# A hybrid attention block on Trainium2: x loaded with features first, the first norm's factor applied to the products

## The chip, the cores and the metric

The kernel runs on one core of one Trainium2 chip. The metric is the device time of one execution in microseconds (us). Of the kernel before, three runs were timed: median 1287.97 us, from 1284.92 to 1291.63. One more execution was taken with the profiler; its own time was 1289.89 us.

## The reference

x has 1024 tokens of 1024 features. What is computed, cut to what matters here:

```
h    = x * rsqrt(mean(x*x, features) + eps) * norm_mix        # first RMSNorm
proj = h @ w_in                                               # 1024 x 3384
qa, ka, va, qi, ki, wi, qb, kb, vb, gdown, ogate = split(proj)
score = sum_h relu(qi_h . ki) * wi_h ; keep the 256 best keys of each query (block causal)
o_a  = softmax(qa . ka + bias, over the kept keys) @ va       # 8 heads of 64
o_b  = gated linear attention of qb, kb, vb with gates from gdown; RMSNorm; * silu(ogate)
x    = x + concat(o_a, o_b) @ w_out
x    = x + (silu(n(x) @ w_gate) * (n(x) @ w_up)) @ w_down     # n: second RMSNorm
out  = RMSNorm(x) * norm_final
```

The factor rsqrt(...) is one number per token and `norm_mix` is one number per feature, so the product of a token's row with `w_in` can be scaled by the token's factor before or after the matmul.

## The kernel before

Every product that must be exact in fp32 is made of three matmuls of a fast fp32 form: an operand is split into a high part (ScalarE, a rounding copy) and a low part (the difference, VectorE or GpSimd), and `mm3` (lines 371 to 374) issues high x high, high x low, low x high. SBUF is handed out in 41 pages of 4 KB per partition, PSUM in four banks (`ps`) and two double banks (`pl`); further small buffers are `hp` and `kb`.

The order of the work is written by a planner, `Flow` (lines 139 to 228), that runs while the program is built. Each piece of work is a thread (a generator) with a rank. It yields what it waits for (an event, a slot, a planned time `At(t)`) or an engine with a cost in ns. The planner always takes the request that can start earliest on its engine; among those within 20 ns it takes the thread of lowest rank. It then lets that thread emit its instruction. The planned times are used for this order alone: on the chip each engine runs its instructions in the order in which they were emitted, each waiting for its real operands. DMAs are all issued by SyncE (SP), in their emitted order too.

The start (lines 405 to 429) issues x in eight tiles of 128 tokens (512 KB each), an identity matrix, the first norm's weight, and the columns of `w_in` for ki, wi and gdown, gathered into one page `wms` by three strided DMAs. Then:

- `first_norm` (482): sum of squares of a token tile (ScalarE or VectorE), the factor (GpSimd), and x scaled in place (VectorE, line 489).
- `hidden` (505): TensorE transposes each 128x128 block of scaled x (line 522). `split_hidden` (492) turns each 128 features x 512 tokens into a page `hT` with high and low part (lines 496 and 498), times `norm_mix`.
- `small_weights` (531) splits `wms` into `wm`.
- `main` (2271) orders TensorE: `misc(0)`, `index_queries(0)`, `misc(1)`, `index_queries(1)`, and then the projections `proj_t` and `proj_f`: vb, og, qkb, qa, va, qa, ka. The number in brackets is the half of the tokens. Results leave PSUM through the functions `evac_...`.
- Beside the projections run `scores` and `choose` (the index scores and a bit by bit search for the 256th score, on VectorE and ScalarE), `bias`, `decays` and `gla`; after ka the softmaxes, the output projection, the FFN.

Weights come through the class `Weights` (lines 231 to 322): three staging buffers `st` (256 KB each), a DMA into a free one, the high part by ScalarE (line 257) into a page, the low part by GpSimd (line 262), which frees the buffer. `Weights.load()` fetches into the staging buffers at once, outside the planner; nothing calls it in the kernel before. `Weights.flow` hands what is staged to the planner's threads, without a planned landing time; a fetch made inside the planner gets one:

```python
for st in self.staged:                            # line 284, when the planner's clock is 0
    staged.put(st)
...
staged.put(self.fetch(), 3200)                    # line 295, in loads()
...
st = yield staged                                 # lines 299 to 302, in highs(), rank 5
yield self
yield ACT, act(HB) + 42
split.put((st, self.high(st)))
```

Of the kernel before, what the change touches and what calls it, by code (L numbers as in the profile page):

```python
# [58 lines left out]
def dve(n):  # L59
    return n / 0.96 + 68  # L60
# [265 lines left out]
def block_kernel(ctx: ExitStack, tc: tile.TileContext, a: dict, out: bass.AP, dbg=None):  # L326
# [78 lines left out]
    xs = {}  # L405

    def load_x(i):
        xs[i] = page([P, D], F32, "x")
        nc.sync.dma_start(xs[i], x[i * P:(i + 1) * P, :])

    load_x(0)
    mats = cst.tile([P, 6, P], F32, name="mats")
    nc.sync.dma_start(mats[:, 0:1, :], a["c_mats"][:, 0:1, :])
    ident, tri, flip, cmask = (mats[:, i, :] for i in range(4))
    cmi = mats[:, 4:6, :].rearrange("p a n -> p (a n)").bitcast(I32)
    load_x(1)
    nrm = cst.tile([P, 2, KT], F32, name="nrm")
    wms = page([P, KT, P], F32, "wms")
    nc.gpsimd.memset(wms, 0.0)
    wv = w_in.rearrange("(k p) n -> p k n", p=P)  # L420
    with nc.allow_non_contiguous_dma("small"):
        nc.sync.dma_start(nrm[:, 0, :], a["norm_mix"].rearrange("l (k p) -> p (l k)", p=P))
        load_x(2)
        load_x(3)
        nc.sync.dma_start(wms[:, :, 32:72], wv[:, :, C_KI:C_KI + 40])
        nc.sync.dma_start(wms[:, :, 0:32], wv[:, :, C_KI:C_KI + 32])
        nc.sync.dma_start(wms[:, :, 96:112], wv[:, :, C_GD:C_GD + 16])
    for i in range(4, 8):
        load_x(i)

    def more_loads():

        todo = [(mats[:, 1:, :], a["c_mats"][:, 1:, :]), (wgu[96:112, :], w_gu),
                   (bgt, row_bc(a["b_gate"], 256)), (gnb, row_bc(a["gla_norm"], 512)), (tab, a["rel_bias"]),
                   (nrm[:, 1, :], a["norm_ffn"].rearrange("l (k p) -> p (l k)", p=P))]
# [13 lines left out]
    junk_v = cst.tile([P, S], BF16, name="junk_v")  # L449

# [18 lines left out]
    pg = Slots(fl, NPG - NT - 1)  # L469
    hp, kb, ps, pl = (Slots(fl, n) for n in (NHP, NKB, 4, 2))  # L470
    fl.free[DMA] = 16500.0
# [5 lines left out]
    hT = {}  # L477

# [3 lines left out]
    def first_norm(i):  # L482
        yield At((4500.0, 6050.0, 8650.0, 10000.0, 14000.0, 15250.0, 16700.0, 18200.0)[i])
        yield (ACT, act(S) + 140) if i % 2 == 0 else (DVE, dve(S))
        ss = sumsq(xs[i], i % 2 == 0)
        yield POOL, 730
        r = rstd_of(ss, 1, D)
        yield DVE, 660
        nc.vector.tensor_scalar(xs[i], xs[i], r, None, op0=ALU.mult)
        ev("xn", i).set()  # L490

    def split_hidden(hf, d, b, give):
# [3 lines left out]
        nc.scalar.activation(t[:, 0, :], b, AF.Copy, scale=nrm[:, 0, d:d + 1])  # L496
        yield DVE, dve(HB) + 60
        nc.vector.scalar_tensor_tensor(t[:, 1, :], b, nrm[:, 0, d:d + 1], f32(t[:, 0, :]),
                                       op0=ALU.mult, op1=ALU.subtract)
        if give is not None:  # L500
            give.give()
        hT[d, hf] = t
        ev("hT", d, hf).set()

    def hidden(hf):

        step = KT if hf == 0 else 2
        for d0 in range(0, KT, step):
            bs = []
            if hf == 0:  # L510
                for _ in range(4):
                    yield ps
                    bs.append((bank("tp"), ps))
            while len(bs) < step:
                yield pl
                w = wide("tp")
                bs += [(w[:, :HB], None), (w[:, HB:], pl)]
            for j in range(4):
                yield ev("xn", hf * 4 + j)
                for d in range(d0, d0 + step):  # L520
                    yield PE, pe(P, 2)
                    nc.tensor.transpose(bs[d - d0][0][:, j * P:(j + 1) * P], xs[hf * 4 + j][:, d * P:(d + 1) * P],
                                        ident)
            for d in range(d0, d0 + step):
                fl.spawn(split_hidden(hf, d, *bs[d - d0]), 0.01 * d)
        pg.give(n=4)
# [4 lines left out]
    def small_weights():  # L531
        yield At(11200.0)
        for _ in range(2):
            yield pg
        yield ACT, act(S)
        wm.extend(page([P, KT, P], F32R, "wm") for _ in range(2))
        nc.scalar.activation(wm[0], wms, AF.Copy)
        yield DVE, dve(S)
        nc.vector.tensor_tensor(wm[1], wms, f32(wm[0]), op=ALU.subtract)
        pg.give()  # L540
        ev("wm").set()

    def evac_misc(hf, b):
        o = slice(hf * HB, (hf + 1) * HB)
        if hf == 0:
            for _ in range(2):
                yield pg
            kw.extend((page([P, S], F32R, "K4"), page([P, S], F32, "wg")))
        K4, wg = kw
        yield ACT, act(HB)  # L550
        nc.scalar.activation(K4[0:64, o], b[0:64, :], AF.Copy)
        yield DVE, dve(HB)
        nc.vector.scalar_tensor_tensor(K4[64:128, o], b[0:64, :], 1.0, f32(K4[0:64, o]),
                                       op0=ALU.mult, op1=ALU.subtract)
        yield ACT, act(HB)
        nc.scalar.activation(wg[64:128, o], b[64:128, :], AF.Copy)
        ps.give()
# [4 lines left out]
    def misc(hf):  # L562
        yield ps
        yield ev("wm")
        b = bank("misc")
        for k in range(KT):
            yield ev("hT", k, hf)
# [55 lines left out]
    def index_queries(hf):  # L623
# [3 lines left out]
        for _ in range(2):  # L627
# [1729 lines left out]
```

## Time and profile before

| what | value |
|---|---|
| median of three runs | 1287.97 us (1284.92 to 1291.63) |
| profiled execution | 1289.89 us, span 1288.1 us |
| TensorE (PE) busy | 1243.2 us, 97% of the span |
| VectorE (DVE), ScalarE (ACT), GpSimd (POOL) busy | 933.7, 600.6, 394.5 us |
| TensorE's mean granted clock | 0.985 |
| DMA | 232 MB, 180 GB/s over the span |

The span runs from the first to the last instruction; the execution's own time is 1.8 us more. TensorE has a granted clock of 1.00 or 0.50 (2.4 or 1.2 GHz); a window's number is the mean. An idle gap is shown in square brackets with the instruction that ended it.

### The profile page before, as it was taken

To read this page: it belongs to the slowest core of one execution; us is meant where nothing else is said; L and a number is where in the kernel's file an instruction comes from. 1 tells how busy PE (TensorE), PEld (TensorE's weight loads), DVE (VectorE), ACT (ScalarE), POOL (GpSimd) and SP (SyncE) were. 2 spreads that over 40 slices of the span, in tenths; PEclk is the share of its full clock that TensorE was granted. 3 is DMA by queue.
4 is the path that set the end of the run, shared out by engine and by line. 5 is a ranking of instruction groups with operands and counts; after the bars stand their busy time and mean duration, and the time that the engine had idled before them with its cause. 6 is when DMAs were issued, how large, how long until landed. Compare 5 with 4: busy or idle time off the path is not lost. (4 is left out here: it accounts for less than half of the span.)

```text
span 1288.1 us, 17923 instructions
## 1 busy us (share of the span) xinstructions
PE 1243.2 (97%) x6074; PEld 1022.6 (79%) x6074; DVE 933.7 (72%) x1739; ACT 600.6 (47%) x1113; POOL 394.5 (31%) x375
## 2 busy tenths in 40 slices
PE   6999999999999999899989999999999999999997
PEld 5878878767787998778868787878888888888885
DVE  6389988979964998843688887768778653335875
ACT  4467777634524787621344444444444332222333
POOL 5324335523401544310103334334333120000340
PEclk8999999979999999999989999999999999999999
DMA  6653221334563437683015777767665479555664
GB/s 212 191 150 123 74 74 42 131 138 152 178 221 100 114 85 201 190 270 129 34 61 184 273 245 258 254 246 261 229 219 205 133 258 379 180 196 190 225 238 164
DMA packets 124909, 232.06 MB, mean 180 GB/s; under 512 B 14297, under 2 KB 72465, under 8 KB 124817
## 3 DMA queue, kind: packets, MB, share of 16 engines
q1 hardware_dynamic: 124816, 230.91, 54.4%
q8 instruction: 48, 0.79, 0.3%
q14 instruction: 45, 0.36, 0.1%
HBM read 148.02 MB, written 82.85 MB: 179 GB/s over the span
## 5 line engine op out<-in xcount | busy, mean ns | idle before, releaser
L1626 POOL TENSOR_TENSOR w<-raw,w 128x512 fp32r<-128x512 f32 x60 | 85.3, 1424 | 214.2 <-ACT w L1766 182.3
L1766 ACT ACTIVATE w<-raw 128x512 fp32r<-128x512 f32 x132 | 81.4, 626 | 54.3 <-DMA d_wd<-wd 15.0
L760 DVE TENSOR_SCALAR_CACHE_REDUCE junk_v<-acc,thr 128x768 bf16<-128x768 f32 (+3 forms) x128 | 103.7, 810 | 2.0
L262 POOL TENSOR_TENSOR w<-st,w 128x512 fp32r<-128x512 f32 x52 | 73.4, 1422 | 75.5 <-ACT w L257 73.3
L767 ACT ACTIVATE junk_a<-acc,thr 128x1024 bf16<-128x1024 f32 x64 | 73.4, 1146 | 46.2 <-DVE thr L784 37.5
L2102 DVE TENSOR_TENSOR da<-U,da 128x512 fp32r<-128x512 f32 x54 | 43.1, 799 | 53.7 <-ACT da L2100 53.5
L2100 ACT ACTIVATE da<-U 128x512 fp32r<-128x512 f32 x54 | 33.7, 630 | 98.8 <-PE da L2156 33.2
L372 PE MATMUL pj<-w,hT 128*128 128x512 f32 x192 | 79.2, 412 | 0.0
L2031 ACT ACTIVATE wd<-wd 128x512 fp32r<-128x512 f32 x77 | 48.3, 629 | 62.1 <-DMA d_wd<-wd 28.1
L373 PE MATMUL pj<-w,hT 128*128 128x512 f32 x192 | 75.9, 395 | 0.0
L374 PE MATMUL pj<-w,hT 128*128 128x512 f32 x192 | 75.8, 395 | 0.0
L372 PE MATMUL pf<-hT,w 128*128 128x512 f32 x192 | 75.8, 395 | 0.0
L1347 POOL TENSOR_SCALAR pb<-pb,sume 128x384 f32<-128x384 f32 (+3 forms) x64 | 47.7, 751 | 89.9 <-DVE sume L1345 74.1
L374 PE MATMUL pf<-hT,w 128*128 128x512 f32 x192 | 74.8, 389 | 0.0
L373 PE MATMUL pf<-hT,w 128*128 128x512 f32 x192 | 74.8, 389 | 0.0
L1807 PE MATMUL fb<-hc,w 128*128 128x512 f32 x176 | 69.5, 395 | 3.9 <-DVE gt L1842 2.5
L1808 PE MATMUL fb<-hc,w 128*128 128x512 f32 x176 | 69.2, 393 | 3.8 <-DVE hc L1629 3.8
L1808 PE MATMUL fc<-hc,w 128*128 128x512 f32 x176 | 69.5, 395 | 2.4 <-DVE hc L1629 2.4
L1807 PE MATMUL fc<-hc,w 128*128 128x512 f32 x176 | 69.1, 392 | 0.4 <-DVE gt L1861 0.4
L2156 PE MATMUL da<-db,da 128*128 128x512 f32 x176 | 68.7, 390 | 0.7 <-DVE da L2102 0.7
L1626 POOL TENSOR_TENSOR wd<-wd 128x512 fp32r<-128x512 f32 x33 | 49.8, 1511 | 63.7 <-ACT wd L2031 55.9
L2154 PE MATMUL da<-db,da 128*128 128x512 f32 x176 | 68.6, 390 | 0.6 <-ACT da L2100 0.6
(315 smaller groups left out, 3643.7 us busy)
## 6 DMA issues: line engine op xcount, KB each, us to landing
d_wd<-wd SPq DMA_DIRECT2D x77, 512.0 KB, 3.5
db<-d_wd SPq DMA_DIRECT2D x77, 512.0 KB, 4.3
st<-w_in SPq DMA_DIRECT2D x52, 256.0 KB, 2.8
raw<-w_ffn_gate SPq DMA_DIRECT2D x22, 512.0 KB, 5.2
raw<-w_ffn_up SPq DMA_DIRECT2D x22, 512.0 KB, 4.5
wd<-w_ffn_down SPq DMA_DIRECT2D x44, 256.0 KB, 4.8
d_ux<-gt SPq DMA_DIRECT2D x9, 512.0 KB, 2.6
d_uy<-gt SPq DMA_DIRECT2D x9, 512.0 KB, 3.5
```

What stands on the lines that cost most here:

```text
L262: (eng or self.nc.gpsimd).tensor_tensor(w[:, 1, :], st, f32(w[:, 0, :]), op=ALU.subtract)
L372: mm(ps, lh, rh, start=first, stop=False)
L373: mm(ps, lh, rl, start=False, stop=False)
L374: mm(ps, ll, rh, start=False, stop=last)
L760: v.tensor_scalar(junk_v[:, :w], acc[ts[i]], col, float(S - TOPK), op0=ALU.is_ge, op1=ALU.subtract, accum_out=cnt[:, i:i + 1])
L767: nc.scalar.activation(junk_a[:, :NA[t]], acc[t], AF.Sign, bias=thf[:, nv:], scale=-1.0, accum_out=cnt[:, nv:])
L1626: nc.gpsimd.tensor_tensor(dst, src, high, op=ALU.subtract)
L1766: nc.scalar.activation(w4[:, 0], src, AF.Copy)
L1807: mm(b, w[:, 0, kk], h[:, 0, :], start=first, stop=False, skip_group_check=True)
L1808: mm(b, w[:, 0, kk], h[:, 1, :], start=False, stop=False, skip_group_check=True)
L2154: mm(bs[t], l[:, 0, tt], r[:, 0, :], start=first, stop=False, skip_group_check=True)
L2156: mm(bs[t], l[:, 1, tt], r[:, 0, :], start=False, stop=last, skip_group_check=True)
```

## The change

x is given to the kernel a second time, transposed (`c_xt`, features first), the small weights are given already gathered (`c_wm`), and both norm weights as rows (`c_norms`). The pages `xT` are split straight into `hT`, times `norm_mix`; there are no transposes and no scaling of x before the products. The tokens' factors are made later, from x in its old layout, which is still loaded. They are applied where results leave PSUM: as a per-partition scale where tokens are rows (`evac_t`, `evac_va`), and by a multiplication with `R` where tokens are columns. `R` holds the factors of all tokens along the free axis, the same in every partition; `rows` makes it with eight plain fp32 matmuls of a diagonal and the identity. Three weight tiles are fetched by `W.load()` at the start.

```diff
+    def load_xt(k, hf):
+        if k % 2 == 0:
+            t = page([P, 2, HB], F32, "xT")
+            xT[k, hf], xT[k + 1, hf] = t[:, 0, :], t[:, 1, :]
+        nc.sync.dma_start(xT[k, hf], a["c_xt"][k * P:(k + 1) * P, hf * HB:(hf + 1) * HB])
...
+    load_xt(0, 0)
+    nc.sync.dma_start(nrm, a["c_norms"])
+    load_wm(0)
+    for k in range(1, 4):
+        load_xt(k, 0)
+    load_wm(1)
+    for k in range(4, KT):
+        load_xt(k, 0)
+    nc.sync.dma_start(mats[:, 0:1, :], a["c_mats"][:, 0:1, :])
+    W.load()
...
-        yield At(26000.0)
+        yield ev("x", NT - 1)
...
-    fl.free[DMA] = 16500.0
+    fl.free[DMA] = 12000.0
     W.flow(fl, pg, R_W)
...
+    def split_hidden(k, hf):
+        if hf == 0:
+            yield At(4500.0 + 650.0 * (k + (k > 3)))
+        else:
+            yield ev("xt", k)
         yield pg
         yield ACT, act(HB) + 42
         t = page([P, 2, HB], F32R, "hT")
-        nc.scalar.activation(t[:, 0, :], b, AF.Copy, scale=nrm[:, 0, d:d + 1])
+        nc.scalar.activation(t[:, 0, :], xT[k, hf], AF.Copy, scale=nrm[:, 0, k:k + 1])
...
+    def load_tokens():
+        W.limit = 4
+        for k in range(KT):
+            if k % 2 == 0:
+                yield pg
+            yield DMA, 650
+            load_xt(k, 1)
+            ev("xt", k).set(2500)
+        for i in range(NT):
+            yield pg
+            yield DMA, 1300
+            xs[i] = page([P, D], F32, "x")
+            nc.sync.dma_start(xs[i], x[i * P:(i + 1) * P, :])
+            ev("x", i).set(2500)
+        W.limit = 8
...
+    def rows():
+        yield pl
+        w = wide("rows")
+        for hf in range(2):
+            yield hp
+            m = half([P, 4, P], F32, "rcol")
             for j in range(4):
+                i = 4 * hf + j
+                yield ev("rs", i)
+                yield DVE, 250
+                nc.vector.tensor_scalar(m[:, j, :], ident, 0.0, rs[:, i:i + 1], op0=ALU.mult, op1=ALU.add)
+                yield PE, 350
+                mm(w[:, i * P:(i + 1) * P], m[:, j, :], ident, start=True, stop=True)
+            hp.give()
+            yield ACT, act(HB)
+            o = slice(hf * HB, (hf + 1) * HB)
+            nc.scalar.activation(R[:, o], w[:, o], AF.Copy)
+            ev("R", hf).set()
+        pl.give()
...
+    def small_weights(i):
+        yield At((5150.0, 7750.0)[i])
...
     def evac_misc(hf, b):
+        yield ev("R", hf)
+        yield DVE, dve(HB)
+        nc.vector.tensor_tensor(wg[:, o], b, R[:, o], op=ALU.mult)
+        ps.give()
         yield ACT, act(HB)
-        nc.scalar.activation(K4[0:64, o], b[0:64, :], AF.Copy)
+        nc.scalar.activation(K4[0:64, o], wg[0:64, o], AF.Copy)
...
     def index_queries(hf):          # half 1 now takes a double bank (pl), not two of ps
     def evac_qi(hf, c, b):          # multiplies by R first, then splits the SBUF copy
...
     def evac_qa(hf, c, b):
-        nc.scalar.activation(t[:, 0, :], b, AF.Copy, scale=-0.125)
-        yield DVE, dve(HB)
-        nc.vector.scalar_tensor_tensor(t[:, 1, :], b, -0.125, f32(t[:, 0, :]), op0=ALU.mult, op1=ALU.subtract)
-        ps.give()
+        nc.vector.scalar_tensor_tensor(q, b, -0.125, R[:, hf * HB:(hf + 1) * HB], op0=ALU.mult, op1=ALU.mult)
+        ps.give()
+        yield ACT, act(HB)
+        nc.scalar.activation(t[:, 0, :], q, AF.Copy)
+        yield POOL, pool2(HB)
+        nc.gpsimd.tensor_tensor(t[:, 1, :], q, f32(t[:, 0, :]), op=ALU.subtract)
...
     def evac_qkb(hf, c, b):
-        nc.scalar.activation(dst[i][:, o], b, AF.Copy, scale=0.125 if c < 2 else 1.0)
+        nc.vector.scalar_tensor_tensor(dst[i][:, o], b, 0.125 if c < 2 else 1.0, R[:, o], op0=ALU.mult, op1=ALU.mult)
...
     def evac_ka(hf, c, b):
+        nc.vector.tensor_tensor(kf, b, R[:, o], op=ALU.mult)
+        ps.give()
         yield ACT, 2 * act(HB)             # two high parts, now from kf in SBUF
...
+            nc.vector.tensor_tensor(k[q, o], kf[r, :], f32(k[r, o]), op=ALU.subtract)
...
+    for i in range(2):
+        fl.spawn(small_weights(i), -1.5)
+    for hf in range(2):
+        for k in range(KT):
+            fl.spawn(split_hidden(k, hf), -1 + hf + 0.01 * k)
+    fl.spawn(load_tokens(), 6)
     for i in range(NT):
+        fl.spawn(first_norm(i), 0.2 + 0.01 * i)
+    fl.spawn(rows(), 0.4)
+    fl.spawn(free_rows(), 1)
```

`first_norm` now waits for `ev("x", i)` and ends with the factor in `rs`; `free_rows` gives R's page back after the last evacuation that reads it.

## Rows read from the trace of the kernel before

**Rows 1.** Section 1 of the page: busy us, share of span, instructions.

```profile
PE 1243.2 (97%) x6074; PEld 1022.6 (79%) x6074; DVE 933.7 (72%) x1739; ACT 600.6 (47%) x1113; POOL 394.5 (31%) x375
```

**Rows 2.** Waits of TensorE: waiter <- releaser: us in total, times, longest.

```profile
PE misc L372 <- DVE hT L498: 2.5, 1, 2.5
...
PE lg L1324 <- DVE mn L1337: 3.1, 2, 2.9
...
PE pk L1102 <- DVE att L1121: 2.9, 1, 2.9
```

**Rows 3.** Windows: busy us of each engine, granted clock, DMA share, GB/s.

```profile
core 0: us, PE busy (x) PEld busy (x) DVE busy (x) ACT busy (x) POOL busy (x), PEclk, DMA share, GB/s
...
0.00:8.54 8.54, 0.00 (x1) 0.01 (x1) 2.08 (x4) 2.43 (x3) 3.98 (x10) 1.00 0.70 230
...
13.00:18.00 5.00, 2.45 (x16) 2.10 (x16) 4.23 (x6) 3.75 (x8) 2.21 (x5) 0.90 1.01 402
...
17.61:23.75 6.14, 6.14 (x15) 4.79 (x16) 6.14 (x9) 5.18 (x10) 3.09 (x5) 0.50 0.32 105
...
250.00:260.00 10.00, 5.91 (x34) 3.89 (x33) 9.89 (x24) 5.71 (x12) 3.97 (x4) 1.00 0.34 117
...
260.00:280.00 20.00, 20.00 (x99) 13.49 (x100) 12.43 (x36) 5.79 (x10) 3.20 (x4) 0.66 0.21 75
```

**Rows 4.** Timeline of TensorE: start us, us, engine, line, operation, count.

```profile
17.61 0.79 PE L372 MATMUL misc<-hT,wm 128*128 128x512 f32 x1 [2.55 <-DVE hT L498]
...
31.63 1.31 PE L522 MATMUL tp<-mats,x 128*128 128x128 f32 x10 [0.43 <-DVE x L489]
...
34.97 1.06 PE L522 MATMUL tp<-mats,x 128*128 128x128 f32 x8
...
35.79 0.48 PE L372 MATMUL misc<-hT,wm 128*128 128x512 f32 x1
...
52.42 0.39 PE L372 MATMUL pj<-w,hT 128*128 128x512 f32 x1
...
227.24 1.05 PE L1028 MATMUL bc<-mats,la 128*128 128x128 f32 x8
...
228.05 0.48 PE L372 MATMUL pf<-hT,w 128*128 128x512 f32 x1
```

**Rows 5.** Timeline of SyncE's DMA issues, start of the program.

```profile
0.72 0.40 SPq L409 DMA_DIRECT2D x<-x  x1
1.18 0.42 SPq L413 DMA_DIRECT2D mats<-c_mats  x1
...
12.06 15.66 SPq L247 DMA_DIRECT2D st<-w_in  x6
```

**Rows 6.** Timeline of ScalarE: its first wait for x.

```profile
4.52 1.06 ACT L460 ACTIVATE junk_a<-x 128x1024 bf16<-128x1024 f32 x1 [2.52 <-DMA x<-x]
```

**Rows 7.** Groups of instructions by line: count, busy us, mean ns, idle before.

```profile
L257 ACT ACTIVATE w<-st 128x512 fp32r<-128x512 f32 x68 | 41.6, 629 | 9.9 <-DMA st<-w_in 5.3 <-DMA st<-w_out 4.3
...
L262 POOL TENSOR_TENSOR w<-st,w 128x512 fp32r<-128x512 f32 x52 | 73.4, 1422 | 75.5 <-ACT w L257 73.3 <-PE pj L374 1.7 <-PE pf L374 0.2
...
L867 DVE SCALAR_TENSOR_TENSOR spillq<-pf,spillq 128x512 fp32r<-128x512 f32 x8 | 5.2, 684 | 0.3 <-ACT spillq L865 0.2
```

**Rows 8.** Timeline of VectorE and GpSimd: L784 alone, then beside GpSimd.

```profile
250.01 0.15 DVE L784 SCALAR_TENSOR_TENSOR thr<-bit,thr 128x3 int32<-128x3 int32 x1
...
256.08 1.47 POOL L888 TENSOR_TENSOR spillv<-spill,spillv 128x512 fp32r<-128x512 f32 x1
...
256.32 1.24 DVE L784 SCALAR_TENSOR_TENSOR thr<-bit,thr 128x3 int32<-128x3 int32 x1
```

**Rows 9.** Line 829, the finished masks: duration ns, first and last start.

```profile
L829 DVE TENSOR_SCALAR acc<-sign x6: 347/588/1664, 257.5 to 368.8; 128x1024 f32<-128x1024 bf16 x2, 128x384 f32<-128x384 bf16 x1, 128x768 f32<-128x768 bf16 x1, 128x512 f32<-128x512 bf16 x1
```

**Rows 10.** Timeline of VectorE where the softmaxes begin.

```profile
402.60 0.56 DVE L1337 CUSTOM_DVE_ANT_0 pb<-lg,acc 128x384 f32<-128x384 f32 x1 [7.42 <-PE lg L1331]
...
405.17 2.79 DVE L1257 SCALAR_TENSOR_TENSOR K<-pf,K 64x512 fp32r<-64x512 f32 x4
```

More of the change, by code (lines that the diff above doesn't have):

```diff
@@ L449, in block_kernel @@
     junk_v = cst.tile([P, S], BF16, name="junk_v")
+    rs = cst.tile([P, NT], F32, name="rs")
     def rstd_of(ss, n, width):
@@ L502, in split_hidden @@
[L502 to L517, printed above, removed]
-            for j in range(4):
[L519 to L526, printed above, removed]
@@ L529, in block_kernel @@
-    wm, kw = [], []
[L531 to L541, printed above, removed]
+        hT[k, hf] = t
+        if k % 2:
+            pg.give()
+        ev("hT", k, hf).set()
@@ new lines, in load_tokens, with first_norm @@
+    def load_tokens():
[13 more added lines that the diff above has]
+        W.limit = 8
+    def first_norm(i):
+        yield ev("x", i)
+        yield (ACT, act(S) + 140) if i % 2 == 0 else (DVE, dve(S))
+        ss = sumsq(xs[i], i % 2 == 0)
+        pg.give()
+        yield POOL, 730
+        r = small([P, 1], F32, "rstd", 4)
+        nc.gpsimd.tensor_scalar(r, ss, 1.0 / D, EPS, op0=ALU.mult, op1=ALU.add)
+        nc.gpsimd.tensor_tensor(rs[:, i:i + 1], r, mhalf[:, 0:1], op=ALU.pow)
+        ev("rs", i).set()
@@ new lines, in block_kernel @@
+    R = page([P, S], F32, "rows")
+    def rows():
[4 more added lines that the diff above has]
+            m = half([P, 4, P], F32, "rcol")
+            for j in range(4):
+                i = 4 * hf + j
[10 more added lines that the diff above has]
+        pl.give()
@@ new lines, in free_rows @@
+    def free_rows():
+        for hf in range(2):
+            for c in range(4):
+                yield ev("ka", hf, c)
+                yield ev("qa", hf, c)
+                yield ev("qk", hf, c)
+        pg.give()
+    wm, kw = [], []
+    def small_weights(i):
+        yield At((5150.0, 7750.0)[i])
+        if i == 0:
+            for _ in range(2):
+                yield pg
+            wm.extend(page([P, KT, P], F32R, "wm") for _ in range(2))
+        o = slice(4 * i, 4 * i + 4)
+        yield ACT, act(HB)
+        nc.scalar.activation(wm[0][:, o, :], wms[:, o, :], AF.Copy)
+        yield DVE, dve(HB)
+        nc.vector.tensor_tensor(wm[1][:, o, :], wms[:, o, :], f32(wm[0][:, o, :]), op=ALU.subtract)
+        if i:
+            pg.give()
+        ev("wm", i).set()
@@ L626, in index_queries @@
         bs = []
-        for _ in range(2):
-            yield ps
-            bs.append(bank("qi"))
+        if hf == 0:
+            for _ in range(2):
+                yield ps
+                bs.append(bank("qi"))
+        else:
+            yield pl
+            w = wide("qi")
+            bs = [w[:, :HB], w[:, HB:]]
         for k in range(KT):
@@ L1247, in evac_ka @@
         yield ev("ka page", c)
+        yield hp
+        yield DVE, dve(HB)
+        kf = half([P, HB], F32, "kf")
+        nc.vector.tensor_tensor(kf, b, R[:, o], op=ALU.mult)
+        ps.give()
         yield ACT, 2 * act(HB)
@@ L2307, in main @@
         yield from down()
+    for i in range(2):
+        fl.spawn(small_weights(i), -1.5)
+    for hf in range(2):
+        for k in range(KT):
+            fl.spawn(split_hidden(k, hf), -1 + hf + 0.01 * k)
+    fl.spawn(load_tokens(), 6)
     for i in range(NT):
[L2310 to L2313 removed]
+        fl.spawn(first_norm(i), 0.2 + 0.01 * i)
+    fl.spawn(rows(), 0.4)
+    fl.spawn(free_rows(), 1)
     fl.spawn(more_loads(), 2)
@@ L2340, in _constants, with _layouts @@
     }
+def _layouts(inputs):
+    w = np.asarray(inputs["w_in"])[0].reshape(KT, P, -1).transpose(1, 0, 2)
+    wm = np.zeros((P, KT, P), np.float32)
+    wm[:, :, 0:32] = w[:, :, C_KI:C_KI + 32]
+    wm[:, :, 32:72] = w[:, :, C_KI:C_KI + 40]
+    wm[:, :, 96:112] = w[:, :, C_GD:C_GD + 16]
+    gains = [np.asarray(inputs[n])[0].reshape(KT, P).T for n in ("norm_mix", "norm_ffn")]
+    return {
+        "c_xt": np.ascontiguousarray(np.asarray(inputs["x"])[0].T),
+        "c_wm": wm,
+        "c_norms": np.ascontiguousarray(np.stack(gains, axis=1)),
+    }
 def kernel(**inputs):
@@ L2349 @@
     arrays.update(_constants())
+    arrays.update(_layouts(inputs))
     aps = {n: nc.dram_tensor(n, v.shape, mybir.dt.from_np(v.dtype), kind="ExternalInput").ap()
```

95 lines of the change are left out of this document (36 added, 59 removed).

## The prediction

> **What bounds the kernel now.** I read the page's busy shares first: TensorE is busy for 1243.2 of 1288.1 us [rows 1], so all other engines only matter where they make it wait or slow. Next the waits of TensorE and the windows: some 45 us of idle time, in few places, and each longer gap is followed by a stretch at half clock. The head is the largest: the first projection matmul starts at 17.61 us, after a last wait of 2.55 us for `hT` [rows 4], and the next 6.14 us run at a granted clock of 0.50 [rows 3]. From there to the first matmul of vb (`pj`, 52.42 us) TensorE is full but for 0.43 us before a batch of transposes [rows 4]. Behind that the notable gaps are 2.9 us at `pk` for `att` in the stretch 250 to 260 us, and 2.9 us at `lg` where the softmaxes begin [rows 2]. So I count on TensorE's timeline: when does the first matmul start, what lies between it and `pj`, and which later gaps change.
>
> **The first matmul.** Before, its chain is x, sum of squares, factor, scaling, transposes, split. Now it is transposed x, `norm_mix` and half the small weights, then one split each. The data would allow an early start: x's first tile of 0.524 MB is read at 4.52 us [rows 6], a tile now is half that, and small weights and `norm_mix` come right behind; split and first matmul would follow at about 6 us.
>
> I don't expect that, because of the order on ScalarE. `W.load()` puts three tiles into staging before the planner starts. `flow` hands them over with no landing time, so for the planner they are there at 0. The first three high parts (L257) therefore can start at 0, 0.58 and 1.16 us of planned time; the first `split_hidden` is held until 4.5 and `small_weights` until 5.15. The planner takes the earliest, so these three stand first in ScalarE's order. On the chip they wait for the weights, which are the last of the first 15 DMAs, and all splits stand behind them.
>
> When does the third land? Ahead of it and with it: 8 tiles of x and 3 of weights of 0.262 MB, 2 parts of small weights of 0.262 MB, identity and norms 0.07 MB: 3.48 MB. Issuing is no limit: 15 issues at 0.46 us (0.72 to 1.18) [rows 5] end at 7.6 us. With 0.524 MB at 4.5 us and then the rate of large rows, 402 GB/s in the stretch 13 to 18 us [rows 3]: 4.5 + 2.96/0.402 = 11.9 us. Then on ScalarE the third high part, the first split and half of the small weights, 0.63 us each (L257) [rows 7]: 13.8, with hops 14.0 us. VectorE's low parts (0.68 us) [rows 7] are ready for the second and third matmul. So the first matmul moves from 17.61 to 14.0: **-3.6 us**. Bounds: 402 is the fastest stretch here; at the 230 GB/s of the first 8.54 us [rows 3], which hold the start and strided loads, the start would be at 4.5 + 12.9 + 2.1 = 19.5, +1.9. I take the fast end, since the transfers are now of its kind (long rows, none strided).
>
> The Trainium skill ("DMA: Bandwidth & Descriptors", section Where 436 GB/s comes from) says that HBM gives a core about 358 GB/s, and that this binds for HBM to SBUF. By that, as an estimate, the third tile lands at 12.8 and the gain is 2.7; the row shows 402 for such loads, and the row decides.
>
> From the first matmul on: per 128 features ScalarE needs 0.63 us, TensorE at half clock three matmuls, and before it ran 15 in 6.14 us [rows 3], 1.23 us for three. So it isn't starved, and it warms up in the same time: no change.
>
> **From the first matmul to `pj`.** Before: 52.42 - 17.61 = 34.8 us. Out go the 32 transposes of the second half, four times eight at 35.79 - 34.97 = 0.82: 3.3 us, and the wait of 0.43 [rows 4]. In come the 8 fp32 products of `rows`: four such take 228.05 - 227.24 = 0.81, so 1.6 us [rows 4]. About as many breaks in the stream as before, 6 against 8; 0.2. Sum **-1.9 us**; bounds -3.7 (products free in a gap) and 0 (each costs twice). `pj` then starts at 46.9.
>
> **What could be late there.** SP's order is x half 0, three weight tiles, then three more weight tiles (planned at 12.0 us, rank 5 before rank 6), x half 1, the token tiles. The three wait for a free buffer, hence for GpSimd's low parts: 11.2 + 3 x 1.42 [rows 7] = 15.5 us, and everything behind waits with them, as the six fetches of L247 held SP for 15.66 us before [rows 5]. Half 1 (2.1 MB) is there by 23 us, needed from 28 (14.0 + the old 8.5 of `misc(0)` and 5.7). A seventh fetch holds the last of half 1 and the token tiles until GpSimd's fourth low part, about 21; the token tiles (4.2 MB) then land by 35, the last factor follows at 37, and the product of its tile stands at some 88% of `index_queries(1)`, near 44: 7 us of cover. R's first half is made near 39, and the first two banks for `pj`, held until the multiplication with R, come free by 42. If this cover went, TensorE would wait at `rows` or at `pj`; that is a rival. The evacuations that wait for R hold up VectorE's and ScalarE's order behind them (scores, weights of vb), which need the products of `index_queries(1)` anyhow.
>
> **Behind `pj`.** The multiplications with R add on VectorE 2 (misc), 4 (qi), 8 (qkb) and 8 (ka) of about 0.68 us [rows 7], 15 us, and 8 diagonals, below 2; the 8 scalings of x are gone. qa keeps its number on VectorE and adds 8 subtractions of 1.42 on GpSimd. ScalarE loses as many copies as qkb and misc drop. PSUM banks are held shorter (one operation, not two). VectorE's long work beside the projections is the search; its last mask starts at 368.8 [rows 9] and the first softmax needs one at 402.60 [rows 10]: 33 us of cover for 15, so nothing, and the full 15 if the cover were gone. One place isn't covered: at 405.17 four low parts of ka take 2.79 us while TensorE waits for a softmax's bank [rows 2, 10]. Two multiplications more in that burst: **+1.4 us**; bounds 0 (they fall into the idle time before) and 2.9 (the gap doubles). Moving qa's low part to GpSimd has a price: L784 takes 0.15 us alone and 1.24 beside a GpSimd subtraction [rows 8]. Eight of them delay VectorE by 0 to 9 us, under the same cover; I take 0.
>
> A rule against the change is in the Trainium skill ("SBUF — State Buffer", section SBUF: two separate sides): a VectorE operation with two SBUF inputs and a GpSimd operation exclude each other for a whole instruction. The low parts of qi and ka change from a PSUM input to two SBUF inputs and so become exposed; as an estimate each could wait up to 1.4 us. The row of L784 agrees; no row shows these operations in the new form.
>
> **Sum.** -3.6 - 1.9 + 1.4 = -4.1 us. Against the profiled execution: 1289.9 - 4.1 = 1285.8. That execution lies 1.9 above the median of the runs, so for a median I take 1288.0 - 4.1 = **1283.9 us**, own range 1280 to 1288 from the bounds.
>
> **Rivals.**
> - *ScalarE isn't held up* (chance 0.10): first matmul at 6 us, -11.6 instead of -3.6, less about 0.5 where half 1 now arrives just in time: 1276.4. For it: the start would then follow the transfers. Against: the order worked out above.
> - *A later gap closes* (0.14): in 250 to 260 us TensorE is idle for 10.0 - 5.9 = 4.1 us, and the next 20 run at a clock of 0.66 [rows 3], which loses 20 x 0.34 = 6.8. The planner's order changes everywhere, and if VectorE is then in time at `pk`: 1283.9 - 10.9 = 1273.0. Against: VectorE gets more work, not less.
> - *One more such gap* (0.14), the slower side: VectorE, 9.89 us busy of 10 in that stretch [rows 3], comes later to `att` or another operation that TensorE's fixed order waits for, through the added multiplications and GpSimd's subtractions. It decides once TensorE waits long enough for its clock to fall: 0.43 us at 31.63 did not do it, the gaps in 250 to 260 did. Price 10.9: 1294.8.
> - *The products wait for R* (0.10): if the token tiles land some 11 us later, TensorE waits 4 at `rows`, and the head's gain is spent: 1288. For it: 4.2 MB more to load, behind two blocked fetches. Against: 7 us of cover.
> - The forecast: 0.52.
>
> **How the numbers follow.** A measurement of this kernel tells a change from none at about 0.5%, 6.4 us: faster is below 1281.5, slower above 1294.4. Faster: 0.10 + 0.14 + a fifth of the forecast's 0.52 (0.10) = 0.34. Slower: 0.09 of the third rival's 0.14, and 0.01 elsewhere: 0.10. The rest, 0.56, is within. The range takes in the first two rivals and most of the third: 1272 to 1293.
>
> **What would show it.** Right: ScalarE's first operations after its table load are three high parts ending near 12.5 us, with all splits behind them; TensorE's first matmul at 13 to 15.5; 32 to 34 us from there to `pj`; no wait at `rows`; last mask well before the first softmax. Wrong: splits on ScalarE from 4 us on; a gap of TensorE at `rows` or at the first `pj`; a gap with half clock in another place than 250 to 280 us, or none there. A change of the total beyond 6 us that isn't in the first 50 us would make the prediction wrong in its core.

## The result, and the profile after

The changed kernel took 1299.27 us (median of four runs, 1297.59 to 1301.23); the kernel before, beside it, 1286.45 us (the three runs named above and a fourth of 1281.27). The ratio is 1.0107, 95% interval 1.0076 to 1.0139: slower, where 1283.9 us was forecast and the range ended at 1293. The profiled execution took 1297.59 us, its span is 1295.8.

Section 1 of the page of the changed kernel answers to [rows 1]. TensorE is busy for 6.4 us less (64 transposes fewer, eight products of `rows` more), while the span is 7.7 us longer: its idle time grew by 14 us.

```profile
PE 1236.8 (95%) x6026; PEld 1014.1 (78%) x6026; DVE 952.2 (73%) x1762; ACT 601.0 (46%) x1106; POOL 406.7 (31%) x382
```

Where it grew is read from windows cut at landmarks of TensorE's order: the first projection matmul (`pj`), the first `pf`, the first `lg` (softmaxes), the first `oa` (output projection), the first `da` (last part of the FFN). Columns as in [rows 3]. The kernel before:

```profile
0.00:52.42 52.42, 40.62 (x208) 34.72 (x209) 27.84 (x38) 27.51 (x47) 30.25 (x36) 0.93 0.64 187
52.42:163.12 110.70, 109.92 (x487) 88.32 (x486) 96.11 (x182) 76.28 (x123) 37.02 (x28) 1.00 0.46 132
163.12:401.82 238.70, 234.60 (x1230) 182.22 (x1229) 189.80 (x460) 121.03 (x212) 83.47 (x75) 0.97 0.40 129
401.82:514.04 112.22, 107.30 (x791) 100.36 (x790) 99.62 (x275) 87.67 (x213) 54.42 (x74) 0.98 0.50 131
514.04:1069.37 555.33, 540.27 (x2440) 444.00 (x2439) 398.71 (x616) 226.46 (x414) 155.70 (x132) 0.99 0.60 206
```

The changed kernel:

```profile
0.00:49.66 49.66, 32.57 (x158) 26.44 (x159) 27.11 (x41) 24.86 (x41) 22.70 (x30) 1.00 0.78 259
49.66:165.98 116.32, 110.87 (x491) 88.44 (x491) 92.73 (x169) 77.78 (x124) 43.41 (x32) 1.00 0.47 138
165.98:404.41 238.43, 232.61 (x1234) 180.60 (x1232) 206.41 (x493) 122.32 (x210) 94.39 (x82) 0.99 0.40 129
404.41:521.49 117.08, 109.46 (x788) 101.40 (x786) 102.95 (x277) 88.53 (x213) 55.22 (x74) 0.97 0.48 127
521.49:1077.14 555.65, 540.81 (x2440) 444.15 (x2439) 400.67 (x616) 225.81 (x414) 157.06 (x132) 0.99 0.60 205
```

The head gains 2.8 us. The stage behind it loses 5.6 and the softmax stage 4.9. The third stage looks unchanged, but the execution of before spent part of it at half clock [rows 3]: its mean granted clock there is 0.97, and 3% of 238.7 us are 7.2. In the re-planned kernel before (n1, below) it is 233.0 us long, so there, too, some 5 us are lost.

The head on ScalarE, answering to [rows 6], is as forecast in kind: three high parts of staged weights, then the first split. They waited 10.95 us, to 12.95, where the third weight tile was forecast to land at 11.9.

```profile
12.95 2.01 ACT L257 ACTIVATE w<-st 128x512 fp32r<-128x512 f32 x3 [10.95 <-DMA st<-w_in]
14.86 0.70 ACT L491 ACTIVATE hT<-xT,nrm 128x512 fp32r<-128x512 f32 x1
```

SyncE, answering to [rows 5]: the fetches of L247 hold it to 18.2 us, and the token tiles are issued behind the second half of transposed x and a seventh fetch, from 23.67 on.

```profile
7.16 11.05 SPq L247 DMA_DIRECT2D st<-w_in  x6
...
23.67 5.12 SPq L512 DMA_DIRECT2D x<-x  x8
```

TensorE's timeline, answering to [rows 4]: the first matmul at 16.14 (before 17.61), `pj` at 49.66 (before 52.42), and the last product of `rows` (two matmul records each) only behind it.

```profile
16.14 0.80 PE L372 MATMUL misc<-hT,wm 128*128 128x512 f32 x1 [16.14 <-ACT wm L568]
...
49.42 0.49 PE L541 MATMUL rows<-mats,rcol 128*128 128x128 f32 x2
49.66 0.47 PE L372 MATMUL pj<-w,hT 128*128 128x512 f32 x1
...
50.44 0.38 PE L541 MATMUL rows<-mats,rcol 128*128 128x128 f32 x2
```

TensorE's waits from 52 us on, answering to [rows 2]. The index scores (`dots`) now wait in places; the wait at `pk` has grown from 2.9 to 3.9, and in the softmaxes those at `lg` from 3.1 to 3.5 and at `av` from 0.6 to 2.6.

```profile
PE dots L745 <- DMA qst<-d_qi: 2.3, 1, 2.3
PE dots L745 <- ACT relu L748: 2.3, 2, 1.9
...
PE pk L1155 <- DVE att L1174: 3.9, 1, 3.9
...
PE lg L1382 <- DVE mn L1395: 3.5, 3, 2.7
PE av L1442 <- DVE pt L1433: 2.6, 4, 1.9
```

The last pair of `dots` starts at 136.96 us, in the kernel before at 122.55:

```profile
122.55 0.62 PE L697 MATMUL dots<-K,qst 128*128 128x512 f32 x2
```

```profile
136.96 0.61 PE L745 MATMUL dots<-K,qst 128*128 128x512 f32 x2
```

The search behind the scores ends late by more: the last mask, at 368.8 before [rows 9], is at 389.4. Of the 33.8 us between it and the first `pb`, 15.8 are left.

```profile
L877 DVE TENSOR_SCALAR acc<-sign x6: 361/518/695, 267.0 to 389.4; 128x1024 f32<-128x1024 bf16 x2, 128x384 f32<-128x384 bf16 x1, 128x768 f32<-128x768 bf16 x1, 128x512 f32<-128x512 bf16 x1
```

VectorE where the softmaxes begin, answering to [rows 10]. Two multiplications with R for ka now stand ahead of the first `pb`; the four low parts (L1315) follow before the third `pb`.

```profile
403.93 1.37 DVE L1304 TENSOR_TENSOR kf<-pf,rows 128x512 f32<-128x512 f32 x2 [6.64 <-PE pf L374]
405.21 0.55 DVE L1395 CUSTOM_DVE_ANT_0 pb<-lg,acc 128x384 f32<-128x384 f32 x1
...
406.62 2.84 DVE L1315 TENSOR_TENSOR K<-kf,K 64x512 fp32r<-64x512 f32 x4
```

### The profile page after: what moved, and what is told of

Read it like the earlier page. It is cut to its first block, busy times and chain, and to the rows that moved or that the text cites. A ratio compares the mean times of both kernels' runs of the same rounds, so it can differ in the third digit from the quotient of the medians.

```text
span 1295.8 us, 17872 instructions
## 1 busy us (share of the span) xinstructions
PE 1236.8 (95%) x6026; PEld 1014.1 (78%) x6026; DVE 952.2 (73%) x1762; ACT 601.0 (46%) x1106; POOL 406.7 (31%) x382
## 5 line engine op out<-in xcount | busy, mean ns | idle before, releaser
L808 DVE TENSOR_SCALAR_CACHE_REDUCE junk_v<-acc,thr 128x512 bf16<-128x512 f32 (+3 forms) x128 | 103.5, 809 | 2.2
L1865 PE MATMUL fa<-hc,w 128*128 128x512 f32 x176 | 68.9, 392 | 1.8 <-ACT gt L1892 1.8
L1687 DVE TENSOR_TENSOR w<-raw,w 128x512 fp32r<-128x512 f32 x72 | 54.5, 762 | 20.3 <-ACT w L1824 20.2
```

What stands on the lines that cost most here:

```text
L808: v.tensor_scalar(junk_v[:, :w], acc[ts[i]], col, float(S - TOPK), op0=ALU.is_ge, op1=ALU.subtract, accum_out=cnt[:, i:i + 1])
L1687: nc.vector.tensor_tensor(dst, src, high, op=ALU.subtract)
L1865: mm(b, w[:, 0, kk], h[:, 0, :], start=first, stop=False, skip_group_check=True)
```

## The experiments

All ratios are against the kernel before on the same chip (its medians there: 1284.0 to 1285.3 us). "R's page" is one of the 41 pages: the changed kernel holds it from the start until after ka. Not all sets ran on the same chip, so where kernels of different sets are compared, the difference of their ratios is given as well.

**First set: the head, R's lateness, the multiplications, the planner.**

e1, the staged weights get a planned landing time, so that the splits come first on ScalarE:

```diff
-            staged.put(st)
+            staged.put(st, 11000.0)
```

> The changed kernel, with one edit: the three weight tiles staged at the start get a planned landing time of 11 us, so that ScalarE splits x first. All theories: ScalarE's first split near 4 us, TensorE's first matmul at 5.5 to 7 us, not 16.1. Theory R (the loss comes from the tokens' factors being late: scores, masks and linear attention start later than TensorE's order wants): the token tiles land no earlier, so TensorE waits at the products of rows or at its banks, the scores start no earlier than 55 us, and the total stays within 4 us of the changed kernel's 1299. Theory H (the late first matmul is what costs): the 9 us are kept to the end, total 1288 to 1291.

1300.57 us, 1.0116 [1.0086, 1.0146]. The first matmul came at 6.2 us and `pj` at 47.2, and nothing of it reached the end: TensorE then waited 3.2 us at `rows`, and 2.9 and 1.9 at `dots`. The late start of TensorE alone wasn't what cost the time.

e2, R is ones from the start, without `rows`, so that what R multiplies lacks its tokens' factors:

```diff
     R = page([P, S], F32, "rows")
+    nc.gpsimd.memset(R, 1.0)
+    for hf in range(2):
+        ev("R", hf).set()
...
-    fl.spawn(rows(), 0.4)
```

> The changed kernel with R filled with ones at the start, and without the eight products of rows: the results that R multiplies (index, GLA and attention queries and keys) lack their token's factor; all else, multiplications and loads too, stays. Theory R: the index scores start by 52 us, their waits (5 us in the changed kernel between 60 and 130 us) go, the last mask is 10 us earlier, total 1282 to 1289. Theory M (the added multiplications on VectorE and the longer evacuations cost the time): 1296 or more. Theory O (a changed kernel order makes gaps by chance): anywhere from 1288 to 1302, with gaps at other places.

1289.57 us, 1.0047 [1.0026, 1.0068]: 9.7 us below the changed kernel, 0.60% by the ratios. But the scores are not early, as theory R had it: `dots` start at 59.3 us, not by 52, wait 5.8 us for `qst`, and end 1.7 us earlier than in the changed kernel. Beside the changed kernel's execution, this one is shorter in the head (by 1.9 us), in the third stage (3.9) and in the FFN (3.9), and longer by 3.5 in the stage with the scores. So it isn't shown that R's lateness costs what e2 saves; and with R ready and the transposes gone the kernel is still no faster than before.

e3, the kernel before with all changed evacuations that multiply, by a page of ones:

```diff
-    pg = Slots(fl, NPG - NT - 1)
+    pg = Slots(fl, NPG - NT - 2)
+    R = page([P, S], F32, "rows")
...
+        nc.vector.tensor_tensor(wg[:, o], b, R[:, o], op=ALU.mult)   # misc; so too qi, qa, qkb, ka; a scale by rs in evac_t, evac_va
```

> The kernel before, with the changed kernel's evacuations: every result is multiplied by R or scaled by rs, both filled with ones at the start, so nothing waits for them; the head with its transposes is as before. It computes the same as before. Theory M: 8 to 14 us slower than before (1295 to 1300). Theory R: within 3 us of before's 1286. Theory O: a difference of up to 6 us either way, from gaps at other places than before.

1295.22 us, 1.0082 [1.0051, 1.0114]: with the old head, the old order of loads and no late R, most of the slowdown is there.

n1, the kernel before, re-planned:

```diff
-    fl.free[DMA] = 16500.0
+    fl.free[DMA] = 17000.0
```

> The kernel before, with one planning number changed: the planner takes the DMA queue as free from 17.0 us instead of 16.5. No instruction is added or left out; only the order can change. Theory O: the total moves by 4 us or more either way. Theories R and M: within 2 us of before.

1283.83 us, 0.9996 [0.9977, 1.0015]. This other order alone moves the kernel before by no more than 0.25%. Its third stage, beside the 238.70 us of before's execution:

```profile
163.30:396.34 233.04, 230.10 (x1231) 179.49 (x1229) 188.55 (x460) 121.02 (x212) 83.34 (x75) 0.99 0.41 132
```

**Second set: e3 taken apart.** e4 takes only ka's multiplication into the kernel before, e5 only that of qkb; both hold R's page.

```diff
-            nc.scalar.activation(Ks[2 * c + e][r, o], b[r, :], AF.Copy)      # e4, in evac_ka
+        nc.vector.tensor_tensor(kf, b, R[:, o], op=ALU.mult)
...
+            nc.scalar.activation(Ks[2 * c + e][r, o], kf[r, :], AF.Copy)
...
-        nc.scalar.activation(dst[i][:, o], b, AF.Copy, scale=0.125 if c < 2 else 1.0)   # e5, in evac_qkb
+        nc.vector.scalar_tensor_tensor(dst[i][:, o], b, 0.125 if c < 2 else 1.0, R[:, o], op0=ALU.mult, op1=ALU.mult)
```

> The kernel before with one of the changed evacuations, that of ka: a VectorE multiplication by R (ones, made at the start, on a page of its own), then high and low parts from SBUF. It computes the same. Theory M, in its part for ka: the stage from the first softmax to the first output projection is 3 to 5 us longer than before (it was 112 us before and 116 to 117 in all kernels with this evacuation), total 1287 to 1290 against 1284. If that stage is unchanged, its loss came from elsewhere, and the total stays within 2 us.

> The kernel before with one of the changed evacuations, that of the GLA's queries and keys (qkb): eight multiplications by R (ones) on VectorE in place of eight copies on ScalarE, and R's page. It computes the same. Theory M, in its part for VectorE beside the search: 5.5 us of VectorE work more, masks and linear attention later by 4 to 7 us, and 2 to 5 us on the total (1286 to 1289). If the page that R takes is what costs, this kernel and the one with ka's multiplication both lose the same. No effect: within 2 us of 1284.

e4: 1295.31 us, 1.0085 [1.0052, 1.0117]. e5: 1293.40 us, 1.0052 [1.0019, 1.0084]. One multiplying evacuation costs as much as all of them (e3). And e4 was slower where it had nothing to multiply yet: its last `dots` start at 132.71 us (before 122.55), 240 us ahead of ka's first multiplication, at 372.8. What e3, e4 and e5 share is the page.

```profile
132.71 0.61 PE L713 MATMUL dots<-K,qst 128*128 128x512 f32 x2
```

e6, small weights and norm weights as rows, the rest as before:

```diff
-        nc.sync.dma_start(wms[:, :, 32:72], wv[:, :, C_KI:C_KI + 40])
-        nc.sync.dma_start(wms[:, :, 0:32], wv[:, :, C_KI:C_KI + 32])
-        nc.sync.dma_start(wms[:, :, 96:112], wv[:, :, C_GD:C_GD + 16])
+    nc.sync.dma_start(wms, a["c_wm"])
```

> The kernel before with only the last part of the change: small weights gathered and norm weights as rows, so three strided DMAs, one memset and two strided norm loads go; transposes and the factor before the products stay. All theories: the third and fourth token tile land 1 to 2 us earlier, the first projection matmul at 16 to 17 us, total 0 to 2 us faster than before (1282 to 1284).

1284.81 us, 0.9998 [0.9977, 1.0019]: no effect; the first matmul starts 1.0 us earlier.

e7, the changed kernel with e1's edit and the first four token tiles loaded ahead of the second half of transposed x, so that R is early:

```diff
-    fl.free[DMA] = 12000.0
+    fl.free[DMA] = 8000.0
...
+        yield from tiles(range(4))      # tiles(r) loads the token tiles of r
         for k in range(KT):
             if k % 2 == 0:
                 yield pg
             yield DMA, 650
             load_xt(k, 1)
             ev("xt", k).set(2500)
+        yield from tiles(range(4, NT))
```

> The changed kernel with staged weights given a landing time of 11 us and the loads in another order: token tiles 0 to 3 ahead of the second half of the transposed x, planned from 8 us. It computes the same. Theory R: R's halves are made some 10 us earlier, the scores start before 50 us, nothing waits for rows, vb starts at 43 to 46 us; of the 14 us lost about 8 to 12 come back, total 1286 to 1291. The multiplications (theory M) keep the rest, so it stays above 1284. Theory M alone (R's lateness costs nothing): 1295 or more.

1295.16 us, 1.0088 [1.0058, 1.0118]: the first matmul at 6.2 us, `pj` at 46.9, and most of the slowdown stays, as theory M alone had it.

**Third set: the page.** There is room in SBUF for 4 KB more per partition, so R can have a tile of its own. e8 holds the page in the kernel before and changes no evacuation; e9 is the changed kernel, e10 is e7, e11 is e4, each with R in its own tile:

```diff
-    pg = Slots(fl, NPG - KT // 2 - 2)            # e9
+    pg = Slots(fl, NPG - KT // 2 - 1)
...
-    R = page([P, S], F32, "rows")
+    R = cst.tile([P, S], F32, name="rows")
...
-    fl.spawn(free_rows(), 1)
```

> The kernel before with one page (R, filled with ones, read by nothing) held from the start until after ka; no evacuation is changed. Theory P (what the change costs is mostly the page: with one of 41 pages less beside the projections the index scores run late): 1289 to 1294 us, the scores end near 133 us as in e4 and e5, and the stretch from the first pf to the first lg stays at 233 to 235 if ka's own multiplication is the price there, at 238 if the page is that too. Theory E (the evacuations alone): 1284 to 1286, scores end near 122.

> The changed kernel with R in an SBUF tile of its own instead of one of the 41 pages, so the page stays with the planner; all evacuations as changed. Theory P: 1299 less 5 to 9: 1290 to 1294. Theory E (the multiplications set the price): 1298 to 1301. If the weights landing late and R's lateness for the scores set it, 1297 to 1301 as well, with the same waits of dots.

> e7 (staged weights with a planned landing time, token tiles 0 to 3 loaded before the second half of transposed x) with R in its own tile: the three known costs of the head and the page taken away, ka's multiplication left. Theory P: 1295 less 5 to 9, 1286 to 1290. Theory E: 1294 to 1297.

> The kernel before with ka's multiplication alone, as in e4, but with R in a tile of its own. Tells what of e4's 10.5 us is the page. Theory P: 1288 to 1290 (3.3 to 5 us remain, in the softmax stage). Theory E: 1294 to 1296 as e4.

| kernel | R's page held | us | ratio to before |
|---|---|---|---|
| e8, no multiplication | yes | 1288.46 | 1.0034 [1.0018, 1.0051] |
| e11, ka's multiplication | no | 1284.70 | 1.0014 [0.9995, 1.0034] |
| e4, ka's multiplication | yes | 1295.31 | 1.0085 [1.0052, 1.0117] |
| changed | yes | 1299.27 | 1.0107 [1.0076, 1.0139] |
| e9, changed | no | 1287.38 | 1.0025 [1.0007, 1.0044] |
| e7, changed, R early | yes | 1295.16 | 1.0088 [1.0058, 1.0118] |
| e10, changed, R early | no | 1284.05 | 0.9989 [0.9968, 1.0010] |

In all three pairs some 11 us (10.6, 11.9, 11.1; by the ratios 0.71, 0.82 and 0.99%) go with the page. That is more than P expected (5 to 9), while the page alone (e8) cost less than the 1289 to 1294 of P. The 3.3 to 5 us that P left to ka's multiplication in e11's softmaxes aren't there: that stage takes 111.8 us, before 112.2. The page and ka's multiplication together (0.85%) would then cost more than one by one (0.34 and 0.14%), but the intervals overlap, so that isn't shown.

**Fourth set: where the page costs.** q1 and q2 are e9 with one page kept back from the planner in one stretch each.

```diff
+    def hold():                                  # q1, with one slot fewer at the start
+        yield ev("score", ORDER[-1])
+        pg.give()
...
+    def hold():                                  # q2
+        yield ev("score", ORDER[-1])
+        yield pg
+        for hf in range(2):
+            for c in range(4):
+                yield ev("ka", hf, c)
+        pg.give()
```

> The changed kernel with R in its own tile (e9), and one page kept back from the planner from the start until the last index score is planned. Theory early (the missing page costs where the index scores run): near 1299, scores end near 137 as in the changed kernel. Theory late (it costs later, in the gated attention's search stage and the softmaxes): near 1287 as e9, even if the scores end late. Theory both: 1291 to 1295. If the 12 us between the changed kernel and e9 are only two different orders by chance, no value of these is owed to the page and the two holds do not add up to 12.

> e9 with one page kept back from the planner from the last index score until after ka's evacuations. Theory early: near 1287, first pf to first lg 235 us, lg to oa 111.7. Theory late: near 1299, with lg to oa at 115 to 117 us as in the changed kernel. Theory both: 1291 to 1295.

q1: 1291.39 us, 1.0056 [1.0033, 1.0078], 4.0 above e9. q2: 1296.79 us, 1.0076 [1.0046, 1.0106], 9.4 above. Both, then, and together 13.4 against the 11.9 between e9 and the changed kernel; by the ratios 0.31 and 0.51%, together the same 0.82. Each alone is just clear of its interval. Windows of e9 from the first to the last `dots`, then the third stage and the softmaxes:

```profile
58.07:128.06 69.99, 67.56 (x298) 53.89 (x296) 57.46 (x86) 49.81 (x78) 24.43 (x18) 1.00 0.60 163
...
163.19:398.13 234.94, 230.54 (x1231) 179.44 (x1230) 202.22 (x480) 119.57 (x206) 91.67 (x82) 0.99 0.41 131
398.13:509.86 111.73, 106.58 (x790) 98.73 (x789) 100.61 (x277) 87.32 (x213) 54.53 (x74) 1.00 0.49 131
```

q1, the `dots`:

```profile
59.05:137.95 78.90, 74.25 (x324) 58.77 (x323) 61.02 (x86) 52.45 (x81) 26.06 (x20) 1.00 0.50 149
```

q2, the same three:

```profile
59.07:130.00 70.93, 67.58 (x298) 53.90 (x296) 57.48 (x86) 49.81 (x78) 24.54 (x18) 1.00 0.59 165
...
165.13:406.48 241.35, 236.73 (x1234) 182.76 (x1232) 202.62 (x481) 118.85 (x206) 91.42 (x82) 0.97 0.39 127
406.48:522.09 115.61, 108.00 (x788) 100.09 (x786) 102.81 (x277) 88.31 (x213) 55.03 (x74) 0.99 0.49 128
```

With a page less, the scores take 78.9 us instead of 70.0. Most of this isn't idle time of TensorE (4.7 us instead of 2.4), as the planner writes projections between them (324 matmuls instead of 298), but everything behind the scores starts late. In the changed kernel the same stretch takes 79.4 us, with the page and no multiplication (e8) 75.2, in e11 65.9. In q2's execution the third stage is longer by 6.4 us (4.9 of them at half clock: 3 against 1% of it) and the softmaxes by 3.9. The 4.9 can't be put down to the page alone: they lie at 320 to 340 us (granted clock 0.68 and 0.63), where a wait of 2.1 us at `pk` for `att` stands that e9's execution doesn't have; and q2's ten runs go from 1287.2 us, at a mean clock of 0.996, to 1301.3, at 0.988. In the FFN, where neither holds a page, q1 and q2 are 2.3 and 2.6 us longer than e9; why, no run tells.

The 3.9 can be seen on VectorE. In e9 the planner begins the softmaxes ahead of ka's last product, so the first `pb` run first and the two multiplications stand between them; TensorE's longest wait at `lg` is 0.7:

```profile
398.90 0.56 DVE L1386 CUSTOM_DVE_ANT_0 pb<-lg,acc 128x384 f32<-128x384 f32 x1 [7.21 <-PE lg L1380]
...
400.21 1.28 DVE L1295 TENSOR_TENSOR kf<-pf,rows 128x512 f32<-128x512 f32 x2
```

```profile
PE lg L1373 <- DVE mn L1386: 1.3, 3, 0.7
```

In q2 the order is the changed kernel's, the multiplications first, and the waits of TensorE have the same numbers as there:

```profile
406.00 1.37 DVE L1295 TENSOR_TENSOR kf<-pf,rows 128x512 f32<-128x512 f32 x2 [6.64 <-PE pf L374]
407.29 0.55 DVE L1386 CUSTOM_DVE_ANT_0 pb<-lg,acc 128x384 f32<-128x384 f32 x1
```

```profile
PE lg L1373 <- DVE mn L1386: 3.5, 3, 2.7
PE av L1433 <- DVE pt L1424: 2.6, 4, 1.9
```

p1, the kernel before with 42 pages (`NPG = 42`):

> The kernel before with 42 pages instead of 41 (there is room for one more). If pages limit the scores before too, as 40 against 41 cost 4.4 us (e8), 1281 to 1283; if the kernel before has enough of them, 1284 to 1286.

1283.37 us, 0.9981 [0.9954, 1.0007]: before had about enough pages; one fewer costs, one more gains at most little. It also bounds the story of the softmaxes: that stage took 115.1 us in p1, without a missing page or a multiplication, so its 4 us hang on the order written, which the page is one way to change.

**Last set: the page or the luck of an order?** The changed kernel, e9 and e10 re-planned, by the planner's first DMA time alone (`fl.free[DMA]` 12000 to 10000, and 8000 to 8500):

> The changed kernel with the planner's DMA clock starting at 10.0 instead of 12.0 us: nothing else is edited, but the planner writes another order on every engine. If the missing page sets the time: 1294 to 1301. If the 12 us between the changed kernel and e9 were the luck of two orders: anywhere from 1284 to 1301.

> e9 (R in its own tile) with the same edit of the planner's start. If the missing page sets the time: 1283 to 1291, some 7 or more below the changed kernel with the same edit. If it was the luck of two orders: no such distance.

> e10 (early R, R in its own tile) with the planner's DMA clock starting at 8.5 instead of 8.0 us. Page: 1281 to 1289, no slower than the kernel before by more than 0.4%. Luck of the order: up to 1297 as e7.

n2 took 1294.77 us, 1.0078 [1.0049, 1.0107]; n4 1286.10 us, 1.0000 [0.9974, 1.0026]; n3 1284.07 us, 0.9992 [0.9979, 1.0005]. Re-planning moved them by 4.5, 1.3 and 0.0 us, none of it clear of the intervals, and the distance between with and without the page survives: n2 and n4 are 8.7 us apart, 0.78%.

## Why the prediction was wrong

The step that failed is the list of what the change adds: it counted instructions, DMAs and waits, but not the page that R takes out of the planner's 41 until ka is done. It has no term in the sum. Beside the added multiplications it costs 8.7 to 11.9 us by the medians of the four pairs, 9 to 13 by their ratios; alone, in the kernel before, 0.34%, 4.4 us (e8). By which waits it costs is shown in part: the scores run late (q1), and the softmaxes begin in another order (q2). How much of the rest is half clock that comes and goes stays open.

Forecast (-0.32%) and result (+1.07%) are 1.39% apart, some 18 us. The page is 0.82 of it (e9), a first matmul at 6 us together with an early R another 0.36 (e10 against e9). With both, `pj` starts at 46.2 us, where 46.9 was forecast, and the total is at -0.11% [-0.32, +0.10], with the forecast at the edge of that interval. The prediction's own sign of being wrong in its core was there: a change of more than 6 us that isn't in the first 50 us.

The other steps:

- *First matmul, -3.6 us:* measured -1.5. The order on ScalarE was right; the weights were late. I let 402 GB/s [rows 3] hold from 4.5 us on, but in the changed kernel the DMAs moved 253 to 267 GB/s until 8 us and 373 to 397 from 8 to 12, so the three high parts end at 15.0, not near 12.5. The slow bound (19.5) was too pessimistic.
- *First matmul to `pj`, -1.9:* 33.5 us instead of 34.8, -1.3. Right, but for a wait of 0.9 us for the low part of the small weights.
- *Cover of 7 us for R:* gone. The last product of `rows` stood at 50.44 us, not near 44. The last token tile was there at 39.7, not 35; GpSimd, which has subtractions for weights between the factors, was done with the last factor at 46.5, not 37; and the last three diagonals took VectorE 2.76 us beside such subtractions, where one takes 0.29 otherwise (lines below). TensorE doesn't wait at `rows` but at `dots`, which start at 57.6 as before, though `pj` comes 2.8 earlier. An earlier R with the landing time is worth 0.19% (e7 against the changed kernel) to 0.36% (e10 against e9), 2.4 to 4.6 us; only the second is clear of its interval. So the rival "the products wait for R" was true in kind, in another place.
- *VectorE's 15 us, hidden:* not refuted for the multiplications ahead of ka. All of them cost what ka's alone does (e3 and e4, 1.0082 and 1.0085), and qkb's nothing that can be told (e5 and e8, 1.0052 and 1.0034).
- *ka's burst, +1.4:* not refuted as long as the page is there: e11, +1.8 us (-0.6 to +4.4), though its softmax stage is no longer than before. With the page missing, the multiplications come ahead of the first `pb`, and the softmax stage is 4 us longer.
- *VectorE and GpSimd excluding each other:* the rule that I weighed (the Trainium skill, "SBUF — State Buffer", section SBUF: two separate sides) isn't tested by ka's low parts. With two SBUF inputs they take 687 ns in the mean of 16, in the old form 698 [rows 10]; but GpSimd is idle for the 44 us before 409.75, in which all sixteen lie. Where the two engines meet, there is a price: of qi's two low parts of 128x512, the one that starts beside a GpSimd subtraction takes 957 ns, the other 678, and the diagonals of `rows`, with one SBUF tile and a number per partition as inputs, take 1.31 us instead of 0.29. The sum had 0 for this.

```profile
35.83 1.29 POOL L262 TENSOR_TENSOR w<-st,w 128x512 fp32r<-128x512 f32 x1
35.90 1.31 DVE L539 TENSOR_SCALAR rcol<-mats,rs 128x128 f32<-128x128 f32 x1 [0.44 <-POOL rs L524]
...
39.10 0.29 DVE L539 TENSOR_SCALAR rcol<-mats,rs 128x128 f32<-128x128 f32 x1 [0.71 <-POOL rs L524]
...
46.47 2.81 POOL L262 TENSOR_TENSOR w<-st,w 128x512 fp32r<-128x512 f32 x2
46.80 2.76 DVE L539 TENSOR_SCALAR rcol<-mats,rs 128x128 f32<-128x128 f32 x3
...
409.75 0.59 POOL L1405 TENSOR_SCALAR pb<-pb,sume 128x384 f32<-128x384 f32 x1 [43.99 <-DVE sume L1403]
```

- *"One more such gap", the slower rival (1294.8):* nearest in time and right in sign, wrong in mechanism. The wait at `pk` grew by 1.0 us only, and the third stage lost less to the clock than in before's execution. The 10.9 us of that gap were themselves partly chance: n1 and e6 idle 2.9 us in that stage and lose 2.3 to the clock, where before's execution had 4.1 and 7.2.
- *The range from the bounds, 1280 to 1288:* the bounds as stated add up to -7.3 and +4.8 us, so to 1280.7 and 1292.8.

So what of the change itself? Without its page (e9) it is 0.25% slower than before [0.07, 0.44], and with R early as well (e10) equal to it. e10's `pj` starts 6.2 us earlier than before, but the stage to the first `pf` is then 4.2 us longer (114.9 us; its `dots` start 4.0 earlier only and wait 2.1 for `qst` and 1.3 for `relu`), and the FFN's stage is 558.1 us long, where before, e6 and n1 have 555.3, 554.2 and 551.0. What delays the FFN by some us wasn't tested; the amount is of the size that re-planning moves. No version here beat the kernel before measurably.

## What to carry to other kernels

Count buffers as a cost like instructions: a change that holds one of a planner's buffers for a third of the kernel takes it from every stage in that time, and the price can show where no instruction of the change stands. A stage that becomes slower ahead of the first edited instruction that could matter there (e4) is the sign of it. And when the order is written by a planner, re-plan both versions once before a difference is put down to one of them.

## What the runs showed of the hardware

- The rate of loads at the start: the windows of the changed kernel show 253 to 267 GB/s from 2 to 8 us, and 397 behind; columns as in [rows 3]. Why, no run tells.

```profile
6.00:8.00 2.00, 0.00 (x0) 0.00 (x0) 0.00 (x0) 0.00 (x0) 0.00 (x0) 1.00 0.86 267
8.00:10.00 2.00, 0.00 (x0) 0.00 (x0) 0.00 (x0) 0.00 (x0) 0.00 (x0) 1.00 1.04 397
```

  The Trainium skill ("DMA: Bandwidth & Descriptors", section Where 436 GB/s comes from) gives some 358 GB/s from HBM for a core; the second row is above it, the first well below.

- The granted clock can read 1.00 where the matmuls come at the pace of half clock. In the first stretch of the changed kernel the matmuls of 512 columns start 0.43 us apart, then 0.23, and the window over the first part still reads 1.00; before, 15 in 6.14 us, 0.41 apart, had a reading of 0.50 [rows 3]. Whether the reading lacks something here or another cause set the pace, no run tells.

```profile
19.46 0.63 PE L373 MATMUL misc<-hT,wm 128*128 128x512 f32 x1
19.88 0.63 PE L374 MATMUL misc<-hT,wm 128*128 128x512 f32 x1
...
22.50 0.39 PE L372 MATMUL misc<-hT,wm 128*128 128x512 f32 x1
22.73 0.39 PE L373 MATMUL misc<-hT,wm 128*128 128x512 f32 x1
```

```profile
20.00:22.00 2.00, 2.00 (x6) 1.54 (x5) 2.00 (x4) 1.71 (x4) 0.51 (x1) 1.00 0.99 300
```
